# Odd layer of a two-layer transformer step on one core: operand parts on VectorE, gate products between the projections, od norms behind the mLSTM heads, set-up later, folded mean square

## The chip, the cores and the metric

One NeuronCore of a Trainium2 chip runs the whole program. The metric is the device time of one execution in microseconds (us), median of the runs. Engines: PE (TensorE, matrix products), DVE (VectorE), ACT (ScalarE), POOL (GpSimd), SP (SyncE, which issues most DMAs).

## The reference

640 tokens (128 of a prompt, 512 latent) of 1,024 features go through two layers; x stays in float32.

```python
layer(x, cvec, l):                      # l = 0 even, l = 1 odd
    shift, scale, gate = split(silu(cvec) @ ada_w + ada_b, 3)
    h   = rmsnorm(x, norm_g) * (1 + scale) + shift
    out = mix(h) @ w_out                # even: MLA + GQA heads; odd: mLSTM + differential heads
    return x + gate * out

odd mix:  u = h @ w_in  ->  qm, km, vm, om, gates, zm (mLSTM);  qd, kd, vd, gd (differential)
    hm = rmsnorm(sigmoid(om) * (mlstm forward + backward)) * silu(zm)
    od = rmsnorm(attend(q1, k1, v) - lam * attend(q2, k2, v)) * (1 - lam_init) * silu(gd)
    lam = exp(sum(l0 * l1)) - exp(sum(l2 * l3)) + lam_init
y = rmsnorm(x, final_norm_g)            # after the odd layer
```

The keys, values and mLSTM states of the prompt are outputs too.

## The kernel before

The layers run one behind the other; in each, the input projections, the heads and the output projection follow each other in **stages** (us of the profiled execution): even projections 0 to 205, even attention 206 to 375, even output projection with the start of the odd layer 376 to 452, odd projections K, Q, V1 and VM 452 to 553, differential heads 553 to 674, mLSTM heads 674 to 805, output projection and final norm to 871.

**Three products for one.** A product in near float32 is made of three products of rounded operands (`mm3`, L83 to L85): high part times high part, low times high, high times low. Weights come by `wload` (L67): a DMA into `raw` (512 KB, 3 buffers, L75 issued by SP), a cast to the high part `whi` (L76, on ACT unless told otherwise) and a subtraction for the low part `wlo` (L77, on DVE unless told otherwise). `whi` and `wlo` have 2 buffers each.

**The start of the odd layer** (`mid`). The even output projection (`out_proj`) adds its two column halves to x tile by tile, sums squares on ACT (L934), forms 1/rms (L940, L47 on DVE, L48 on POOL) and calls `after` for each of the five token tiles: scale x (L989), transpose (L997, PE), scale and shift half of it on DVE (L1004, h) and half on ACT (L1002), round to `Hh` (L1005, ACT), subtract for `Hl` (L1007: the first half on DVE, the second on POOL). Then projection **V0** (L1027 on: 5 tiles of 24 products 128x272) needs `Hh` and `Hl` of one tile after the other. Its gate columns are `gt` (L1034).

**The projections** K, Q, V1, VM (`odd_linear`): each 120 products (five tiles, eight pieces of the depth, three products). Before them stands the set-up of lambda (L1050 to L1060), behind V1 the mLSTM gates (`mlstm_gates`, L1224 on, with memsets of `pad`, `zz` and `Q`).

**The differential heads** (`diff`): for each of 4 heads and 5 tiles `front` makes two score tiles (L619), row maximum (L626), exp (L629, ACT), and on DVE the factor f (L1174, L1175) and the difference of the two maps (L1176); `back` transposes it (L1188), copies it (L1190) and multiplies by the values (L1195). Between them run, as filler of the PE, the products of `qk_feat` (L1109, eight weight tiles m = 0 to 7, two accumulators), whose casts and low parts are made on POOL, and the eight parts of the odd layer's output gate (`ada_gate_part`: a load into `raw`, L226, eight products L230 that read `raw` itself, and a copy `gp`, L232, ACT). The row of the gate (`ada_gate_row`, L238 to L248, products L241) comes behind mLSTM head 0.

**The order.** The program text gives the dependencies; a scheduler with a simulated timeline fixes each engine's order when the kernel is built, so a change of the text can move instructions far from where it is written. Pools with a fixed number of buffers make an instruction wait until the buffer's last reader is through. `issue_after` keeps instructions behind a given one.

Of the kernel before, what the change touches and what calls it, by code (L numbers as in the profile page):

```python
# [17 lines left out]
EPS = 1e-6  # L18
# [19 lines left out]
class K:  # L38
# [859 lines left out]
    def out_proj(self, W, L, order, gates, otmp, ps, after, tags, then=None):  # L898

        nc = self.nc  # L900
        self.ada_gate_bc(L, gates)
        acc = {t: ps.tile([128, 512], F32, tag=tags[t], name="acc", bufs=5 if tags[t] == "acc" else 1) for t in range(5)}

        def mm(c, t, m, a=0, b=512):
            for k in range(4 * m, 4 * m + 4):
                oh, ol = self.sp[m, t]
                wh, wl = self.ww[c, k // 2]
                self.mm3(acc[t][:, 0:b - a], oh[:, k % 4], ol[:, k % 4], wh[:, k % 2, a:b], wl[:, k % 2, a:b],
                         k == 4 * order[0], k == 4 * order[1] + 3)

        for t in range(5):
            mm(0, t, order[0])
        if order[0] == 0:
            self.op_rest()
        xt = self.xt
        for c in range(2):
            if c:
                for i in range(4):
                    self.op_load(W, 1, (2 * order[0] + i) % 4, i >= 2 and L == "o")
            for t in range(5):  # L920
                parts = [(0, 256), (256, 512)] if then and c and t == 4 else [(0, 512)]
                for i, (a, b) in enumerate(parts):
                    cs, n = slice(c * 512 + a, c * 512 + b), b - a
                    if c:
                        acc[t] = ps.tile([128, 512], F32, tag="acc", name="acc", bufs=5)
                        mm(1, t, order[0], a, b)
                    mm(c, t, order[1], a, b)
                    g = self.gate[:, 1 if t == 0 else 0]
                    tmp = otmp(t + i)[:, 0:n]
                    nc.vector.tensor_tensor(out=tmp, in0=acc[t][:, 0:n], in1=g[:, cs], op=ALU.mult)  # L930
                    eng = nc.gpsimd if L == "e" and c == 0 else nc.vector
                    eng.tensor_tensor(out=xt[:, t, cs], in0=xt[:, t, cs], in1=tmp, op=ALU.add)
                    junk = self.st.tile([128, 512], mybir.dt.bfloat16, tag="sq", name="junk", bufs=1)
                    nc.scalar.activation(out=junk[:, 0:n], in_=xt[:, t, cs], func=AF.Square,  # L934
                                         accum_out=self.sq2[:, c + i, t:t + 1])
                    if then:
                        then(c, t, xt[:, t], cs)
                    if c == 1:
                        ss = self.st.tile([128, 1], F32, tag="ssq", name="ssq", bufs=6)
                        nc.vector.tensor_tensor(out=ss, in0=ss_ if i else self.sq2[:, 0, t:t + 1],  # L940
                                                in1=self.sq2[:, 1 + i, t:t + 1], op=ALU.add)
                        ss_ = ss
                if c == 1:
                    after(t, xt[:, t], self.rsqrt(ss, 1, 1024))


    def odd(self):
# [33 lines left out]
    def mid(self, S, ps):  # L981
# [5 lines left out]
        def after(t, x, r):  # L987
# [4 lines left out]
            for j in range(2):  # L992
# [10 lines left out]
                    else:  # L1003
                        nc.vector.tensor_scalar(out=h32[:, k], in0=src, scalar1=g, scalar2=b, op0=ALU.mult, op1=ALU.add)  # L1004
                nc.scalar.copy(Hh[:, ks, s], h32)  # L1005
                eng = nc.gpsimd if j else nc.vector
                last = eng.tensor_tensor(out=Hl[:, ks, s], in0=h32, in1=Hh[:, ks, s], op=ALU.subtract)  # L1007
                if not j:
                    self.last = last

        def rest():
            for t in range(5):
# [15 lines left out]
        for t in range(5):  # L1028
# [4 lines left out]
            nc.scalar.copy(self.v0[:, t], acc[:, 0:256])  # L1033
            nc.vector.tensor_tensor(out=self.gt[:, t], in0=acc[:, 256:272], in1=self.rows[:, R_GB:R_GB + 16], op=ALU.add)  # L1034

    def odd_linear(self, M, D, Y0, Gp, ps):
        nc, A, O = self.nc, self.A, self.O
        Hh, Hl = self.Hh, self.Hl
# [8 lines left out]
        nc.scalar.dma_start(ck, A["cdkT"])  # L1047
        nc.gpsimd.memset(v1[:, :, :, 128:129], 1.0)

        lam = self.rows[:, R_LAM:R_LAM + 256]  # L1050
        lt = Gp.tile([128, 64], F32, name="lt")
        ls = Gp.tile([128, 2], F32, name="ls")
        for i in range(2):
            nc.vector.tensor_tensor(out=lt, in0=lam[:, 128 * i:128 * i + 64], in1=lam[:, 128 * i + 64:128 * i + 128],
                                    op=ALU.mult)
            nc.vector.tensor_reduce(out=ls[:, i:i + 1], in_=lt, axis=AX.X, op=ALU.add)
        nc.scalar.activation(out=ls, in_=ls, func=AF.Exp)
        self.nlam = nlam = M.tile([128, 1], F32, name="nlam")
        nc.vector.tensor_tensor(out=nlam, in0=ls[:, 1:2], in1=ls[:, 0:1], op=ALU.subtract)
        nc.vector.tensor_scalar(out=nlam, in0=nlam, scalar1=-LAM_INIT, scalar2=None, op0=ALU.add)  # L1060

        vi = lambda t: 5 if t == 0 else t
        for t in range(5):
# [25 lines left out]
        for nm, n, e in (("o_wK", 512, evk), ("o_wQ", 512, evq), ("o_wV1", 256, ev1), ("o_wVM", 512, evv)):  # L1089
            pieces = [(A[nm][i], A[nm].shape[2]) for i in range(A[nm].shape[0])]  # L1090
            if nm == "o_wVM":
                self.head0 = self.prep_dq(0, Y0, ps), self.prep_dk(0, Y0, ps)
            self.lin_tok(pieces, n, Hh, Hl, range(5), e, ps)
            if nm == "o_wV1":
                r = self.mlstm_gates(M, Gp, ps)
        self.gates = r

    def qk_feat(self, ps):

        nc, A = self.nc, self.A  # L1100
        self.qk = self.st.tile([128, 8, 640], F32, tag="ogx", name="qk", bufs=1)
        for m in range(8):
            wh, wl = self.wload(A["o_wkm" if m % 2 else "o_wqm"][m // 2], 8, 128, cp=nc.gpsimd.tensor_copy, lo_on=nc.gpsimd)
            acc = [ps.tile([128, 512], F32, tag="acc", name="acc", bufs=2) for _ in range(2)]
            for k in range(8):
                for a, b, f, l in ((wh, self.Hh, k == 0, False), (wh, self.Hl, False, False),
# [50 lines left out]
    def diff(self, Y0, Y, ps):  # L1157
# [41 lines left out]
        if True:  # L1199
# [4 lines left out]
            for h in range(4):  # L1204
                for t in [1, 2, 3, 4, 0]:
                    cur = front(h, t, qs, ks)
                    if t == 2 and h < 3:
                        nq = self.prep_dq(h + 1, YY[(h + 1) % 2], ps)
                    if t == 3 and h < 3:
                        nk = self.prep_dk(h + 1, YY[(h + 1) % 2], ps)  # L1210
                    if t in (4, 0):
                        self.ada_gate_part("o", 2 * h + (t == 0), ps, "t1", 1)
                    if pend is not None:
                        back(*pend)
                    pend = cur
                qs, ks = nq, nk
# [109 lines left out]
    def mlstm(self, D, ps):  # L1326
# [361 lines left out]
```

## Time and profile before

| | us |
|---|---|
| median of 3 runs (872.51 to 872.6) | 872.58 |
| the profiled execution | 872.72 |
| span of its instructions | 870.9 |
| outside the span | 1.8 |
| PE busy | 830.3 (95%) |
| DVE busy | 532.4 (61%) |
| ACT busy | 425.6 (49%) |
| POOL busy | 249.8 (29%) |

How to read it: the PE is the engine that is nearly always at work, and the mean clock granted to it is 0.996 of the full one. Its instructions are the same before and after the change, so a change of the time shows as idle time of the PE, or as products at the lower clock, in the stage where it arises.

### The profile page before, as it was taken

To read this page: it belongs to the slowest core of one execution; us is meant where nothing else is said; L and a number is where in the kernel's file an instruction comes from. 1 tells how busy PE (TensorE), PEld (TensorE's weight loads), DVE (VectorE), ACT (ScalarE), POOL (GpSimd) and SP (SyncE) were. 2 spreads that over 40 slices of the span, in tenths; PEclk is the share of its full clock that TensorE was granted. 3 is DMA by queue.
4 is the path that set the end of the run, shared out by engine and by line. 5 is a ranking of instruction groups with operands and counts; after the bars stand their busy time and mean duration, and the time that the engine had idled before them with its cause. 6 is when DMAs were issued, how large, how long until landed. Compare 5 with 4: busy or idle time off the path is not lost.

```text
span 870.9 us, 14357 instructions
## 1 busy us (share of the span) xinstructions
PE 830.3 (95%) x5418; PEld 711.2 (82%) x5418; DVE 532.4 (61%) x1143; ACT 425.6 (49%) x936; POOL 249.8 (29%) x240
## 2 busy tenths in 40 slices
PE   5999999999999998899999999999999999999996
PEld 2778899998788766678888898899988788888786
DVE  3674777324766777535751675377674857676845
ACT  5354356423666866623452235456554656533423
POOL 0010241102755766703320000411310833221121
PEclk9999999999999999999999999999999999999999
DMA  9922222221233112554122213122124222153303
GB/s 343 361 74 73 58 81 79 78 85 52 71 105 117 50 49 74 159 210 142 79 85 102 81 54 109 49 82 84 52 75 135 84 68 69 55 175 113 129 2 121
DMA packets 29641, 88.52 MB, mean 102 GB/s; under 512 B 3752, under 2 KB 6880, under 8 KB 29572
## 3 DMA queue, kind: packets, MB, share of 16 engines
q1 hardware_dynamic: 25904, 83.64, 28.3%
q10 hardware_dynamic: 3668, 3.96, 1.4%
q8 instruction: 43, 0.70, 0.3%
q14 instruction: 26, 0.21, 0.1%
HBM read 80.90 MB, written 6.68 MB: 101 GB/s over the span
## 4 chain that ended last, share of the span: by engine, by line
PE 79%; DVE 7%; POOL 5%; ACT 3%; issue 3%; DMA 2%; SPq 0%; POOLq 0%; ACTq 0%; DVEq 0%
PE acc L83 13%; PE acc L85 13%; PE acc L84 13%; PE acc L120 6%; PE s L619 6%; PE acc L1109 6%; PE o L657 3%; PE t L646 3%; PE pv L1516 2%; PE o L1195 2%; PE ada L186 2%; POOL p L639 1%; PE acc L583 1%; DMA raw<-in_o_wO_dram 1%; PE accA L85 1%
## 5 line engine op out<-in xcount | busy, mean ns | idle before, releaser
L84 PE MATMUL acc<-wlo,Hh 128*128 128x512 f32 (+2 forms) x400 | 149.4, 374 | 0.0
L85 PE MATMUL acc<-whi,Hl 128*128 128x512 f32 (+2 forms) x400 | 148.7, 373 | 0.2 <-DVE Hl L1007 0.2
L83 PE MATMUL acc<-whi,Hh 128*128 128x512 f32 (+2 forms) x400 | 145.6, 380 | 2.4 <-ACT Hh L1005 1.4
L77 DVE TENSOR_TENSOR wlo<-raw,whi 128x1024 fp32r<-128x1024 f32 (+4 forms) x67 | 80.1, 1196 | 94.5 <-ACT whi L76 93.9
L76 ACT CAST whi<-raw 128x1024 fp32r<-128x1024 f32 (+4 forms) x71 | 71.7, 1010 | 128.1 <-PE acc L85 76.1
L626 DVE TENSOR_REDUCE nm<-s 128x1 f32<-128x640 f32 (+1 forms) x104 | 81.0, 779 | 52.1 <-PE s L619 51.2
L639 POOL TENSOR_TENSOR p<-p,rs 128x640 f32<-128x640 f32 x64 | 79.2, 1253 | 95.6 <-issue 52.9
L629 ACT ACTIVATE p<-s,nm 128x640 f32<-128x640 f32 (+1 forms) x104 | 79.4, 765 | 38.4 <-DVE nm L626 36.2
L83 PEld LDWEIGHTS acc<-whi,Hh 128*128 128x128 f32 x400 | 75.5, 190 | 14.6 <-ACT Hh L1005 1.7
L85 PEld LDWEIGHTS acc<-whi,Hl 128*128 128x128 f32 x400 | 76.0, 190 | 13.5 <-DVE Hl L1007 0.4
L84 PEld LDWEIGHTS acc<-wlo,Hh 128*128 128x128 f32 x400 | 76.2, 190 | 12.0 <-DVE wlo L77 0.2
L48 POOL TENSOR_TENSOR rs_r<-rs_h,mhalf 128x1 f32<-128x1 f32 (+4 forms) x39 | 36.9, 950 | 148.8 <-DVE rs_h L47 148.5
L646 PE MATMUL t<-cst,p 128*128 128x128 f32 x320 | 46.9, 276 | 3.1 <-POOL p L639 2.2
L85 PE MATMUL acc<-whi,ol 128*128 128x512 f32 (+1 forms) x124 | 48.0, 387 | 0.0
L84 PE MATMUL acc<-wlo,oh 128*128 128x512 f32 (+1 forms) x124 | 47.8, 387 | 0.0
L83 PE MATMUL acc<-whi,oh 128*128 128x512 f32 (+1 forms) x124 | 47.3, 389 | 0.4 <-DVE z L1418 0.4
L646 PEld LDWEIGHTS t<-cst,p 128*128 128x128 f32 x320 | 36.9, 141 | 8.5 <-POOL p L639 3.6
L651 ACT COPY pT<-t 128x512 f32<-128x512 f32 x56 | 32.0, 587 | 19.1 <-PE t L646 18.5
L632 DVE RECIPROCAL rs<-sm 128x1 f32<-128x1 f32 x104 | 16.6, 159 | 27.3 <-ACT p L629 25.7
L619 PE MATMUL s<-Ka,qh 96*128 96x320 f32 (+1 forms) x128 | 31.6, 329 | 1.7 <-DVE og L127 0.9
L1109 PE MATMUL acc<-Hh,whi 128*128 128x320 f32 x128 | 32.5, 323 | 0.5 <-ACT v L1086 0.5
L1148 POOL TENSOR_TENSOR kdl<-ckd,kdh 128x128 fp32r<-128x128 f32 x8 | 3.6, 461 | 100.9 <-ACT kdh L1147 100.9
(385 smaller groups left out, 1925.0 us busy)
## 6 DMA issues: line engine op xcount, KB each, us to landing
adaw<-in_eada_ss_dram SPq DMA_DIRECT2D x16, 512.0 KB
raw<-in_oada_ss_dram SPq DMA_DIRECT2D x16, 512.0 KB
raw<-in_e_wG_dram SPq DMA_DIRECT2D x8, 512.0 KB
raw<-in_eada_g_dram SPq DMA_DIRECT2D x8, 512.0 KB
raw<-in_e_wO_dram SPq DMA_DIRECT2D x8, 512.0 KB
raw<-in_oada_g_dram SPq DMA_DIRECT2D x8, 512.0 KB
raw<-in_o_wO_dram SPq DMA_DIRECT2D x8, 512.0 KB
xT<-in_xT_dram SPq DMA_DIRECT2D x8, 320.0 KB
```

Of the source, the lines that this page charges most:

```text
L76: (cp or nc.scalar.copy)(hi[:, 0:m], raw[:, 0:m])
L77: (lo_on or nc.vector).tensor_tensor(out=lo[:, 0:m], in0=raw[:, 0:m], in1=hi[:, 0:m], op=ALU.subtract)
L83: mm(out, lhsT=lh, rhs=rh, start=first, stop=False)
L84: mm(out, lhsT=lh, rhs=rl, start=False, stop=False)
L85: self.mark = mm(out, lhsT=ll, rhs=rh, start=False, stop=last)
L120: mm(acc[j][:, 0:320], lhsT=a[:, k], rhs=b[:, k, j * 320:j * 320 + 320], start=f, stop=l)
L619: self.mark = self.nc.tensor.matmul(out[:, j, 0:w], lhsT=q[0:rows, qcols], rhs=k[0:rows, a:a + w], start=i == 0, stop=i == len(passes) - 1)
L626: nc.vector.tensor_reduce(out=nm, in_=s, axis=AX.XY, op=ALU.max, negate=True)
L629: nc.scalar.activation(out=p[:, 0:n].rearrange("p (a b) -> p a b", a=s.shape[1]), in_=s, func=AF.Exp, bias=nm, accum_out=sm)
L639: self.pm = self.nc.gpsimd.tensor_tensor(out=p, in0=p, in1=rs.to_broadcast([128, 640]), op=ALU.mult)
L646: self.nc.tensor.transpose(tp[:, i * 128:i * 128 + 128], p[i][:, k * 128:k * 128 + 128], self.ident)
L1109: nc.tensor.matmul(acc[j][:, 0:320], lhsT=a[:, k], rhs=b[:, k, j * 320:j * 320 + 320], start=f, stop=l)
```

## The change

- `out_proj`: the two-step sum of squares and its scaling (L940, L47) become one `scalar_tensor_tensor` with a constant part that is made ahead (`pre`).
- `mid`: all ten low parts `Hl` are subtracted on DVE.
- Lambda (now a function of its own) and `mlstm_gates` are issued behind the last `Hl`, or behind what that name last held.
- `odd_linear`: the eight gate parts leave `diff` and follow the projections: parts 0 and 1 after K, 2 to 4 after Q, 5 after V1, 6 and 7 after VM; they use the `tp` accumulators (3 buffers). The row of the gate follows VM.
- `qk_feat`: the cast goes from POOL to ACT, the low part from POOL to DVE, and each weight tile is asked for one m earlier.
- `mlstm`: the five `unit` calls (rms norm of `od`) leave the start and follow heads 0, 1 and 2.

```diff
@@ out_proj @@
                     if c == 1:
-                        ss = self.st.tile([128, 1], F32, tag="ssq", name="ssq", bufs=6)
-                        nc.vector.tensor_tensor(out=ss, in0=ss_ if i else self.sq2[:, 0, t:t + 1],
-                                                in1=self.sq2[:, 1 + i, t:t + 1], op=ALU.add)
-                        ss_ = ss
+                        ms = self.st.tile([128, 1], F32, tag="rs_h", name="rs_h", bufs=4)
+                        nc.vector.scalar_tensor_tensor(out=ms, in0=self.sq2[:, 1 + i, t:t + 1], scalar=1.0 / 1024,
+                                                       in1=part if i else pre[:, t:t + 1], op0=ALU.mult, op1=ALU.add)
+                        part = ms
                 if c == 1:
-                    after(t, xt[:, t], self.rsqrt(ss, 1, 1024))
+                    r = self.st.tile([128, 1], F32, tag="rs_r", name="rs_r", bufs=6)
+                    nc.gpsimd.tensor_tensor(out=r, in0=ms, in1=self.mhalf[:, 0:1], op=ALU.pow)
+                    after(t, xt[:, t], r)
+            if c == 0:
...
@@ mid, after @@
-                eng = nc.gpsimd if j else nc.vector
-                last = eng.tensor_tensor(out=Hl[:, ks, s], in0=h32, in1=Hh[:, ks, s], op=ALU.subtract)
-                if not j:
-                    self.last = last
+                self.last = nc.vector.tensor_tensor(out=Hl[:, ks, s], in0=h32, in1=Hh[:, ks, s], op=ALU.subtract)
@@ odd_linear @@
-        lam = self.rows[:, R_LAM:R_LAM + 256]
...
+        with self.tc.issue_after(self.last.ins):
+            self.negated_lambda(M, Gp)
@@ odd_linear, the loop over o_wK, o_wQ, o_wV1, o_wVM @@
             self.lin_tok(pieces, n, Hh, Hl, range(5), e, ps)
+            for i in {"o_wK": (0, 1), "o_wQ": (2, 3, 4), "o_wV1": (5,), "o_wVM": (6, 7)}[nm]:
+                self.ada_gate_part("o", i, ps, "tp", 3)
             if nm == "o_wV1":
-                r = self.mlstm_gates(M, Gp, ps)
+                with self.tc.issue_after(self.last.ins):
+                    r = self.mlstm_gates(M, Gp, ps)
+        self.ada_gate_row("o", ps, "tp", 3)
         self.gates = r
@@ qk_feat @@
+        load = lambda m: self.wload(A["o_wkm" if m % 2 else "o_wqm"][m // 2], 8, 128) if m < 8 else None
+        w = load(0)
         for m in range(8):
-            wh, wl = self.wload(A["o_wkm" if m % 2 else "o_wqm"][m // 2], 8, 128, cp=nc.gpsimd.tensor_copy, lo_on=nc.gpsimd)
+            (wh, wl), w = w, load(m + 1)
@@ diff @@
-                    if t in (4, 0):
-                        self.ada_gate_part("o", 2 * h + (t == 0), ps, "t1", 1)
@@ mlstm @@
-        for t in range(5):
-            self.unit(four(od[:, t]))
...
             self.mlstm_head(X2, ps, h, *self.gates, self.v1, hm, ncl, adv)
-            if h == 0:
-                self.ada_gate_row("o", ps, "it", 1)
+            for t in ((0, 1), (2, 3), (4,), ())[h]:
+                self.unit(four(od[:, t]))
```

What the scheduler makes of it, at three places.

**Place 1, between Q and V1.** The DMA queue of SP, before: `raw` buffers are asked for by the weights of K, Q, V1 and VM one behind the other.

```order
L75 DMA raw<-in_o_wK_dram 128x1024
L75 DMA raw<-in_o_wQ_dram 128x1024 x4
L75 DMA raw<-in_o_wV_dram 128x1024 x2
L75 DMA raw<-in_o_wVM_dram 128x1024 x3
L1271 DMA mxd<-Q 36x640
```

The same queue after the change (`oada_g` are the gate parts; `o_wV` with 128x1024 is V1):

```order
L75 DMA raw<-in_o_wK_dram 128x1024
L226 DMA raw<-in_oada_g_dram 128x1024 x2
L75 DMA raw<-in_o_wQ_dram 128x1024 x4
L226 DMA raw<-in_oada_g_dram 128x1024 x3
L75 DMA raw<-in_o_wV_dram 128x1024 x2
L226 DMA raw<-in_oada_g_dram 128x1024
L75 DMA raw<-in_o_wVM_dram 128x1024 x4
```

And the PE after the change, from the last products of Q (128x512) to the first of V1 (128x256):

```order
L84 MATMUL acc<-wlo,Hh_4402 128x512
L85 MATMUL acc<-whi,Hl_4403 128x512
L230 MATMUL gps<-raw,sc 32x128 x24
L83 MATMUL acc<-whi,Hh_4402 128x256 x5
L84 MATMUL acc<-wlo,Hh_4402 128x256
L85 MATMUL acc<-whi,Hl_4403 128x256
```

Three gate loads now stand ahead of V1's first load in the queue, and the 24 products that read these three buffers stand behind the last product of Q.

**Place 2, DVE in the start of the odd layer**, from the last addition of the even output projection (otmp, xt) of tile 4 on. Before (lt: lambda; pad, zz, Q: mLSTM gates):

```order
L1007 TENSOR_TENSOR Hl_4403<-h_4777,Hh_4402 128x4x128
L930 TENSOR_TENSOR otmp<-acc,gate 128x512
L1054 TENSOR_TENSOR lt<-rows 128x64
L1229 MEMSET pad 128x360
L1253 MEMSET zz 36x640
L1255 MEMSET Q 128x1920
L932 TENSOR_TENSOR xt<-xt,otmp 128x512
L1056 TENSOR_REDUCE ls<-lt 128x1
L1004 TENSOR_SCALAR h_4839<-tp,gso 128x128 x4
```

After:

```order
L1012 TENSOR_TENSOR Hl_4403<-h_4773,Hh_4402 128x4x128
L930 TENSOR_TENSOR otmp<-acc,gate 128x512
L1012 TENSOR_TENSOR Hl_4403<-h_4785,Hh_4402 128x4x128
L932 TENSOR_TENSOR xt<-xt,otmp 128x512
L1010 TENSOR_SCALAR h_4833<-tp,gso 128x128 x4
L940 SCALAR_TENSOR_TENSOR rs_h<-sq_77,pre 128x1
L995 TENSOR_SCALAR xt<-xt,rs_r 128x1024
```

Lambda and the memsets are gone from between the two halves of tile 4's addition; one more `Hl` has come in.

**Place 3, ACT at the change from VM to the differential heads**, after the change (v: the evacuations of VM; gp: parts 6 and 7 of the gate; p: the first exps). Before, the five copies v and the first exp were neighbours.

```order
L1094 COPY v_5087<-acc 128x4x128 x3
L76 CAST whi<-raw 128x1024
L232 COPY gp<-gps 128x128 x2
L629 ACTIVATE p,sm<-s_6051,nm 128x640
L629 ACTIVATE p,sm<-s_6069,nm 128x640
L629 ACTIVATE p,sm<-s_6091,nm 128x640
L76 CAST whi<-raw 128x1024
L1127 ACTIVATE qk<-acc 128x320 x2
```

A cast of `qk_feat` and two gate copies stand between them, and the next cast stands ahead of the copies qk that free the accumulators.

## Rows read from the trace of the kernel before

**Rows 1.** The page, first part: busy time of each engine, its share of the span, instructions.

```profile
PE 830.3 (95%) x5418; PEld 711.2 (82%) x5418; DVE 532.4 (61%) x1143; ACT 425.6 (49%) x936; POOL 249.8 (29%) x240
```

**Rows 2.** Busy time by stretch (start:end, length, then PE, PE's weight loads, DVE, ACT, POOL with their instructions, the granted clock, DMA share, GB/s): the projections K to VM; the differential heads with the start of the mLSTM heads.

```profile
450.00:545.00 95.00, 95.00 (x498) 81.31 (x498) 49.95 (x89) 31.35 (x52) 3.60 (x7) 0.99 0.28 93
545.00:690.00 145.00, 139.16 (x1041) 129.60 (x1039) 94.61 (x194) 80.94 (x191) 42.58 (x33) 1.00 0.24 79
```

**Rows 3.** Timeline of the PE in projection V0: start, duration, engine, line, operation, tiles, shape, count; in brackets the idle time before and what ended it. The transposes shown are tile 4's; the last row is the first product of K.

```profile
432.03 0.28 PE L83 MATMUL acc<-whi,Hh 128*128 128x272 f32 x1
432.15 0.29 PE L84 MATMUL acc<-wlo,Hh 128*128 128x272 f32 x1
...
443.94 1.04 PE L997 MATMUL tp<-cst,xt 128*128 128x128 f32 x8
...
447.40 0.39 PE L83 MATMUL acc<-whi,Hh 128*128 128x272 f32 x1 [1.43 <-ACT Hh L1005]
...
452.54 0.63 PE L83 MATMUL acc<-whi,Hh 128*128 128x512 f32 x2
```

**Rows 4.** Busy time by stretch, columns as in rows 2: two stretches of V0 behind its wait, and one in the even attention.

```profile
448.00:450.00 2.00, 1.87 (x9) 1.87 (x10) 0.08 (x1) 0.08 (x1) 2.00 (x5) 0.60 0.00 0
450.00:452.00 2.00, 2.00 (x11) 2.00 (x11) 1.00 (x1) 1.01 (x2) 0.66 (x2) 0.55 0.00 0
350.00:360.00 10.00, 8.25 (x78) 6.62 (x77) 6.43 (x14) 7.05 (x14) 8.03 (x6) 1.00 0.46 131
```

**Rows 5.** Timeline of DVE in the start of the odd layer.

```profile
432.46 1.80 DVE L1007 TENSOR_TENSOR Hl<-h,Hh 128x512 fp32r<-128x512 f32 x1
...
436.39 1.66 DVE L1255 MEMSET Q<- 128x1920 f32 x1 [0.35 <-issue]
437.98 0.62 DVE L932 TENSOR_TENSOR xt<-xt,otmp 128x512 f32<-128x512 f32 x1
...
440.68 0.69 DVE L1007 TENSOR_TENSOR Hl<-h,Hh 128x512 fp32r<-128x512 f32 x1
441.36 0.75 DVE L989 TENSOR_SCALAR xt<-xt,rs_r 128x1024 f32<-128x1024 f32 x1
```

**Rows 6.** Timeline of SP's DMA queue: the two loads of V1.

```profile
483.15 7.86 SPq L75 DMA_DIRECT2D raw<-in_o_wV_dram  x2
```

**Rows 7.** Timeline of the PE in the differential heads: one gate part and the product behind it.

```profile
571.79 0.64 PE L230 MATMUL gps<-raw,sc 128*32 128x128 f32 x16
572.36 0.56 PE L619 MATMUL s<-kdh,q 128*128 128x320 f32 x2
```

**Rows 8.** The chain of waits that ended last, in its stretch ahead of the odd output projection: start, duration, what.

```profile
794.11 4.59 DMA raw<-in_o_wO_dram
...
799.80 1.24 DVE wlo L77
801.06 3.50 DMA raw<-in_o_wO_dram
```

**Rows 9.** Timeline of the PE: instructions that it had to wait for, in the even attention (first row), the differential heads and the start of the mLSTM heads (last row).

```profile
352.73 0.87 PE L619 MATMUL s<-Kb,q 128*128 128x320 f32 x4 [1.75 <-ACT p L629]
...
553.27 0.41 PE L1109 MATMUL acc<-Hh,whi 128*128 128x320 f32 x1 [0.53 <-ACT v L1086]
...
564.85 0.56 PE L619 MATMUL s<-kdh,q 128*128 128x320 f32 x2 [1.02 <-ACT p L629]
...
568.60 0.56 PE L619 MATMUL s<-kdh,q 128*128 128x320 f32 x2 [0.46 <-DVE q L1138]
...
613.71 0.33 PE L1188 MATMUL t<-cst,p 128*128 128x128 f32 x1 [0.43 <-DVE p L1176]
...
631.96 0.63 PE L1188 MATMUL t<-cst,p 128*128 128x128 f32 x4 [0.35 <-DVE p L1176]
...
633.92 0.65 PE L230 MATMUL gps<-raw,sc 128*32 128x128 f32 x16 [1.22 <-ACT pT L1190]
...
674.55 0.50 PE L83 MATMUL acc<-whi,Hh 128*128 128x512 f32 x1 [1.00 <-ACT qk L1113]
...
691.27 0.49 PE L1516 MATMUL pv<-v,s 128*128 128x129 f32 x2 [1.43 <-DVE s L1498]
```

**Rows 10.** Timeline of POOL in the differential heads: one low part of `qk_feat`.

```profile
583.74 2.40 POOL L77 TENSOR_TENSOR wlo<-raw,whi 128x1024 fp32r<-128x1024 f32 x1
```

**Rows 11.** Timeline of DVE at the same time: one factor f.

```profile
584.38 1.77 DVE L1175 SCALAR_TENSOR_TENSOR f<-rs,nlam,f 128x1 f32<-128x1 f32 x1
```

**Rows 12.** The instructions of L1175 in the differential heads: duration in ns, least, median and greatest.

```profile
L1175 DVE SCALAR_TENSOR_TENSOR f<-rs,nlam,f x20: 208/220/1768, 561.4 to 663.6; 128x1 f32<-128x1 f32 x20
```

**Rows 13.** Timeline of ACT: the five evacuations of VM, and the two places where a cast of a weight stood ahead of the copies qk already.

```profile
549.91 3.31 ACT L1086 COPY v<-acc 128x512 f32<-128x512 f32 x5 [9.82 <-PE acc L85]
...
660.24 1.04 ACT L76 CAST whi<-raw 128x1024 fp32r<-128x1024 f32 x1
...
673.12 1.04 ACT L76 CAST whi<-raw 128x1024 fp32r<-128x1024 f32 x1 [2.02 <-PE acc L1109]
```

**Rows 14.** Timeline of POOL at the start of the mLSTM heads: the norm of `od`.

```profile
678.12 1.01 POOL L48 TENSOR_TENSOR rs_r<-rs_h,mhalf 128x4 f32<-128x4 f32 x1
```

**Rows 15.** The end of the chain of waits that ended last.

```profile
865.66 0.17 DVE ssq L940
865.86 0.17 DVE rs_h L47
```

More of the change, by code (lines that the diff above doesn't have):

```diff
@@ L938, in out_proj @@
                     if c == 1:
-                        ss = self.st.tile([128, 1], F32, tag="ssq", name="ssq", bufs=6)
-                        nc.vector.tensor_tensor(out=ss, in0=ss_ if i else self.sq2[:, 0, t:t + 1],
-                                                in1=self.sq2[:, 1 + i, t:t + 1], op=ALU.add)
-                        ss_ = ss
+                        ms = self.st.tile([128, 1], F32, tag="rs_h", name="rs_h", bufs=4)
+                        nc.vector.scalar_tensor_tensor(out=ms, in0=self.sq2[:, 1 + i, t:t + 1], scalar=1.0 / 1024,
+                                                       in1=part if i else pre[:, t:t + 1], op0=ALU.mult, op1=ALU.add)
+                        part = ms
                 if c == 1:
-                    after(t, xt[:, t], self.rsqrt(ss, 1, 1024))
+                    r = self.st.tile([128, 1], F32, tag="rs_r", name="rs_r", bufs=6)
+                    nc.gpsimd.tensor_tensor(out=r, in0=ms, in1=self.mhalf[:, 0:1], op=ALU.pow)
+                    after(t, xt[:, t], r)
+            if c == 0:
+                pre = self.st.tile([128, 5], F32, tag="pre", name="pre", bufs=1)
+                nc.vector.tensor_scalar(out=pre, in0=self.sq2[:, 0], scalar1=1.0 / 1024, scalar2=EPS, op0=ALU.mult,
+                                        op1=ALU.add)
     def odd(self):
@@ L1034, in mid, with negated_lambda @@
             nc.vector.tensor_tensor(out=self.gt[:, t], in0=acc[:, 256:272], in1=self.rows[:, R_GB:R_GB + 16], op=ALU.add)
+    def negated_lambda(self, M, Gp):
+        nc = self.nc
+        lam = self.rows[:, R_LAM:R_LAM + 256]
+        lt = Gp.tile([128, 64], F32, name="lt")
+        ls = Gp.tile([128, 2], F32, name="ls")
+        for i in range(2):
+            nc.vector.tensor_tensor(out=lt, in0=lam[:, 128 * i:128 * i + 64], in1=lam[:, 128 * i + 64:128 * i + 128],
+                                    op=ALU.mult)
+            nc.vector.tensor_reduce(out=ls[:, i:i + 1], in_=lt, axis=AX.X, op=ALU.add)
+        nc.scalar.activation(out=ls, in_=ls, func=AF.Exp)
+        self.nlam = nlam = M.tile([128, 1], F32, name="nlam")
+        nc.vector.tensor_tensor(out=nlam, in0=ls[:, 1:2], in1=ls[:, 0:1], op=ALU.subtract)
+        nc.vector.tensor_scalar(out=nlam, in0=nlam, scalar1=-LAM_INIT, scalar2=None, op0=ALU.add)
     def odd_linear(self, M, D, Y0, Gp, ps):
@@ L1048, in odd_linear @@
         nc.gpsimd.memset(v1[:, :, :, 128:129], 1.0)
-        lam = self.rows[:, R_LAM:R_LAM + 256]
[L1051 to L1060, printed above, removed]
+        with self.tc.issue_after(self.last.ins):
+            self.negated_lambda(M, Gp)
         vi = lambda t: 5 if t == 0 else t
```

## The prediction, written before the change was run

> **What bounds the kernel now.** I read the page's busy times first: the PE works 95% of the span [rows 1]. The change leaves the PE's instructions as they are, so only its idle time and its slow products can change. The stretches came next: between 450 and 545 us the PE is busy 95.00 of 95.00, so the projections wait for nothing; between 545 and 690 it is idle 145 - 139.16 = 5.8 [rows 2]. Then the PE's timeline, gap by gap, told where it waits in the stages that the change touches: once in V0, with products that follow at a lower clock [rows 3, 4], and some eight times in the differential heads and behind them [rows 9]. For each gap I followed the releaser on DVE, ACT and POOL [rows 5, 10, 13], and for each moved instruction which buffer it waits for and who stands behind it in its queue (the three places above).
>
> **The change part by part.** All sums stand against the profiled execution, 872.72; the median of the runs, 872.58, is 0.14 lower, which I neglect.
>
> *V0: -3.6.* Before, the x addition of tile 4 ends late because lambda and a memset of 1.66 stand ahead of it, so that its scaling starts at 441.36 [rows 5] and its transposes at 443.94 [rows 3]. The PE waits 1.43 for `Hh` at 447.40, and the last 24 products of V0, 447.40 to 452.54, take 5.14 where 24 at 0.125, the step at full clock (432.03 to 432.15), would be 3.0 [rows 3]: 2.1 more, most of it the clock, granted at 0.60 and 0.55 in these two stretches [rows 4]. After, nothing foreign stands ahead of the addition; the largest memset alone, 1.66, exceeds the one extra `Hl`, 0.69 beside an idle POOL [rows 5]. Worked through with these durations tile 4's `Hh` and `Hl` are ready 0.8 before the PE comes to them. I take off both the wait and the slow products: -1.43 - 2.1, or -3.6. Bounds: -3.6 and 0 (rival D). That all `Hl` go to DVE costs nothing while DVE keeps ahead; without that cover each would cost its 0.69.
>
> *From Q to V1: +6.3.* Gate products read `raw` themselves, so that each of parts 2, 3 and 4 holds one of the three `raw` buffers until the PE has run it, and the PE runs it behind Q's last product (place 1). V1's first load waits for part 2. Before, V1's loads left at 483.15 and by 491.01 [rows 6], long before their use. After, counted from Q's last product: a gate part takes 0.57 (571.79 to 572.36), its result 0.64 [rows 7]; the load takes 3.50 alone and 4.59 beside others [rows 8], and since three loads leave within 1.2 us I take the middle, 4.05; the cast on ACT takes 1.04 [rows 13]: V1's first product at 5.7. Parts 3 and 4 keep the PE busy until 1.7, so it idles 4.0. Then five products need the high part only (place 1), 0.6, while the low part takes 1.24 [rows 8]: 0.6 more. That is 4.6 (4.0 with the shorter load, 5.1 with the longer).
> To it comes the clock. Behind the wait of 1.43 in V0 the granted clock was 0.60 and 0.55 over two stretches of 2 us, that is the lower level (1.2 GHz instead of 2.4) for nearly all of the time; it cost (0.40 + 0.45) x 2 = 1.7 [rows 4]. Behind the wait of 1.75 at 352.73 it stayed 1.00 [rows 4, 9]. This wait is more than twice as long as either, so I take the nearer row and 1.7; the bounds are 0 and 2.1. The Trainium skill speaks against the change here: "TensorE: Matmul & The Clock Gate", section "HAM oscillation", tells that a wait for a DMA between groups of products puts the array back to the slow clock, so that the next group starts slow. By that rule the term stays 6.3, and without it 4.6; the trace has one wait on either side.
> K to Q and V1 to VM cost nothing: the loads held by parts 0, 1 and 5 are the third and fourth weight piece of the projection behind, needed some 14 us later. If that cover were gone they would cost the same 4.6.
>
> *From VM to the differential heads: +0.5.* The first score waits until the gate's row is summed, which needs the copies gp of parts 6 and 7; on ACT these stand behind the last of the v copies and behind a cast (place 3). The v copies end at 553.22 [rows 13], some 0.7 behind VM's last product; a cast of 1.04 and two short copies bring it to some 2.3. The PE has 2 x 0.57 [rows 7] and 0.2 of other products, so it idles 1.0, where before it idled 0.53 [rows 9]. Bounds: 0 (the scheduler's cast finds ACT free earlier) and +2.2 (the clock falls).
>
> *Differential heads: +0.6.* On the credit side stands POOL. Its low parts of `qk_feat` take 2.40 [rows 10], and while one runs, a DVE subtraction of two values per partition is stretched: f took 1.77 from 584.38 to 586.15, when POOL's low part, begun at 583.74, ended [rows 10, 11]; the median is 0.22 [rows 12]. The PE's waits that I put down to it are 0.46, 0.43, 0.35 and 1.22 (the last for a pT delayed by f) [rows 9]: -2.4. The 1.02 at 564.85 is ACT's and stays.
> On the debit side the eight casts now go to ACT, each 1.04, directly ahead of the copies qk that free the accumulators, at six borders between weight tiles, with the next exp queued behind. Two rows show what such a cast does: at 660.24 the PE had no wait, at 673.12 it waited 1.00 [rows 9, 13]. At the first border ACT is late already (the 1.02), so it pays 1.04 in full; the other five have 1.7 to 2.2 of other PE work in front of them, against 1.04 + 0.77 of ACT, and are nearer to the first row: 0.4 each, 2.0. The gate parts leave, which frees ACT of eight short copies but takes 8 x 0.57 of filler from the PE; I count that as nothing, covered by the next `qk_feat` products, and up to +1.5 without them. Sum -2.4 + 1.0 + 2.0 = +0.6; bounds -2.4 and +3.6 (all six at 1.0), or +5 with the filler.
>
> *Start of the mLSTM heads: -1.0.* A POOL norm of 1.01 [rows 14] no longer stands ahead of a low part of the first head, whose chain ends in the wait of 1.43 at 691.27 [rows 9]. Bounds: 0 and -1.8; the middle. *Tail: -0.2*: of two DVE steps of the last chain, 0.17 each with the step between [rows 15], one is left.
>
> **Sum:** -3.6 + 6.3 + 0.5 + 0.6 - 1.0 - 0.2 = +2.6, or 872.7 + 2.6 = **875.3**. Its own range, from the bounds of the junction and of the casts, is about 872.8 to 878.5.
>
> **The rivals.**
> *B, POOL's release outweighs the casts (not slower).* If all borders are like 660.24, the differential heads give -2.4 instead of +0.6: 875.3 - 3.0 = 872.3, no change; and if the clock holds between Q and V1 as at 352.73, 870.6, faster. It decides at the slack in front of the accumulators' copies: 1.8 of ACT work against 1.7 to 2.2. For it speaks that DVE lost more to POOL than the PE's waits show (20 f of up to 1.77 [rows 12]); against it the first border. The Trainium skill, "SBUF — State Buffer", section "Who interferes with whom", says that a DVE instruction with two SBUF inputs and a GpSimd instruction that reads SBUF exclude each other on a shared port. The row of 1.77 agrees; by that rule every stretched f goes, which is this rival, 872.3.
> *C, the casts cost in full.* All six borders pay 1.0: +3.6 instead of +0.6, 878.3. ACT is busy only 80.94 of 145 [rows 2], which speaks against it, but each exp is on the way to the PE.
> *D, V0 keeps its wait.* If tile 4 is late again, for `Hl` on a DVE that now makes ten, the 3.6 fall out: 878.9. Only 0.8 of margin speaks against it.
> *E, the loads are not held*, the change doing something other than place 1 shows: 875.3 - 6.3 = 869.0. Against it stands the order itself.
>
> **How the numbers follow.** A measurement of this kernel tells about 0.2%, 1.75 us, from no change: faster is below 870.8, slower above 874.3. The forecast has a chance of 0.50 (0.35 slower, 0.15 within), B 0.27 (0.14 within, 0.13 faster), C 0.10 and D 0.08 (slower), E 0.05 (faster). That makes faster 0.18, same 0.29, slower 0.53. The range from 869.6 to 879.6 leaves out E, a little of B, and the outer bounds of C and D.
>
> **What would show it.** Right: V0 without a wait for `Hh` and with a clock of 1.00; between the last 128x512 product of Q and the first 128x256 one a gap of 4 us ended by the cast `whi`, with a granted clock well under 1 behind it; a wait of about 1 us for the gate's sum before the first score; f near its median everywhere; casts on ACT ahead of qk. Wrong: V1's first load leaving before Q's last product, idle time of the PE in the differential heads under 3 or over 8, or a wait for `Hl` in V0.

## The result, and the profile after

| | us |
|---|---|
| before, median of 4 runs | 872.59 |
| changed kernel, median of 4 runs (879.97 to 880.93) | 880.38 |
| ratio to before, 95% interval | 1.0086 (1.0068 to 1.0103) |
| changed kernel, profiled execution / its span | 880.67 / 878.6 |

Slower by 7.8, where 2.6 was forecast with a range up to 879.6.

The page's busy times after (answers to [rows 1]):

```profile
PE 836.1 (95%) x5418; PEld 714.6 (81%) x5418; DVE 534.6 (61%) x1148; ACT 433.6 (49%) x944; POOL 212.7 (24%) x219
```

The span grew by 7.7, the PE's busy time by 5.8 and its idle time by 1.9 only. With the same instructions, longer busy time means slower products.

From Q to V1, the PE's timeline of the changed kernel:

```profile
505.95 0.40 PE L85 MATMUL acc<-whi,Hl 128*128 128x512 f32 x1
506.27 1.52 PE L230 MATMUL gps<-raw,sc 128*32 128x128 f32 x48
511.89 0.86 PE L83 MATMUL acc<-whi,Hh 128*128 128x256 f32 x5 [4.10 <-ACT whi L76]
513.15 0.58 PE L84 MATMUL acc<-wlo,Hh 128*128 128x256 f32 x1 [0.40 <-DVE wlo L77]
```

SP's queue and ACT at the same place:

```profile
481.08 13.96 SPq L226 DMA_DIRECT2D raw<-in_oada_g_dram  x3
506.98 0.80 SPq L75 DMA_DIRECT2D raw<-in_o_wV_dram  x2
```

```profile
510.79 1.04 ACT L76 CAST whi<-raw 128x1024 fp32r<-128x1024 f32 x1 [2.67 <-DMA raw<-in_o_wV_dram]
```

V1's first load leaves behind Q's last product, where before it left at 483.15 [rows 6]; the PE waits 4.10 and 0.40. Stretches of 2 us behind this wait, and two at the first border of the differential heads (columns as in rows 2):

```profile
512.00:514.00 2.00, 1.60 (x9) 1.39 (x10) 2.00 (x3) 1.05 (x1) 0.00 (x0) 0.71 0.29 117
514.00:516.00 2.00, 2.00 (x11) 2.00 (x11) 2.00 (x4) 0.00 (x0) 0.00 (x0) 0.50 0.84 274
516.00:518.00 2.00, 2.00 (x18) 2.00 (x17) 0.80 (x2) 0.00 (x0) 0.00 (x0) 0.94 0.72 240
```

```profile
578.00:580.00 2.00, 2.00 (x10) 2.00 (x10) 1.82 (x4) 0.88 (x2) 0.00 (x0) 0.50 0.13 51
580.00:582.00 2.00, 2.00 (x14) 2.00 (x13) 0.21 (x3) 0.96 (x2) 0.00 (x0) 0.73 0.00 0
```

The granted clock of 0.71, 0.50 and 0.94 costs (0.29 + 0.50 + 0.06) x 2 = 1.7.

V0 as one stretch (answers to [rows 3, 4]): no wait, full clock, 16.8 from its first product to K's where it took 20.5.

```profile
431.90:449.00 17.10, 17.10 (x139) 17.02 (x138) 12.51 (x29) 9.02 (x21) 2.11 (x6) 1.00 0.08 32
```

The PE where VM ends and at the first border of the differential heads (answers to [rows 9]):

```profile
562.24 0.61 PE L241 MATMUL gsum<-gp,cst 128*32 128x256 f32 x6
563.36 0.62 PE L241 MATMUL gsum<-gp,cst 128*32 128x256 f32 x2 [0.52 <-ACT gp L232]
...
576.45 0.56 PE L619 MATMUL s<-kdh,q 128*128 128x320 f32 x2 [1.80 <-ACT p L629]
```

ACT ahead of that border, and the factor f (answers to [rows 12, 13]):

```profile
573.34 1.05 ACT L76 CAST whi<-raw 128x1024 fp32r<-128x1024 f32 x1 [0.34 <-ACT p L629]
574.29 0.76 ACT L1127 ACTIVATE qk<-acc 128x320 f32<-128x320 f32 x2
574.94 0.68 ACT L1151 CAST q<-qtp 64x640 fp32r<-64x640 f32 x1
575.51 0.80 ACT L629 ACTIVATE p<-s,nm 128x640 f32<-128x640 f32 x1
```

```profile
L1189 DVE SCALAR_TENSOR_TENSOR f<-rs,nlam,f x20: 209/219/222, 572.2 to 673.8; 128x1 f32<-128x1 f32 x20
```

f is at its median everywhere, as forecast; the cast stands ahead of the copies qk and the exp that the PE waits for.

What no step had foreseen is seen in a stretch without any wait. Projection K, before and after:

```profile
470.24 0.39 PE L83 MATMUL acc<-whi,Hh 128*128 128x512 f32 x1
470.47 0.39 PE L84 MATMUL acc<-wlo,Hh 128*128 128x512 f32 x1
470.69 0.39 PE L85 MATMUL acc<-whi,Hl 128*128 128x512 f32 x1
470.92 0.39 PE L83 MATMUL acc<-whi,Hh 128*128 128x512 f32 x1
```

```profile
469.98 0.40 PE L83 MATMUL acc<-whi,Hh 128*128 128x512 f32 x1
470.21 0.40 PE L84 MATMUL acc<-wlo,Hh 128*128 128x512 f32 x1
470.45 0.40 PE L85 MATMUL acc<-whi,Hl 128*128 128x512 f32 x1
470.68 0.40 PE L83 MATMUL acc<-whi,Hh 128*128 128x512 f32 x1
```

Three products take 0.68 before and 0.70 after: a step of 0.2267 against 0.2333 at the same granted clock of 1.00. The 360 products of K, Q and VM make 2.4 of it.

One more fall of the clock stands in the even attention, which the change does not touch: here behind a wait of 1.78, where before it stayed at 1.00 behind 1.75 at the same place [rows 4, 9].

```profile
352.00:354.00 2.00, 1.92 (x9) 1.88 (x10) 0.85 (x2) 1.29 (x4) 2.00 (x2) 0.60 0.01 4
354.00:356.00 2.00, 2.00 (x11) 1.72 (x11) 0.90 (x3) 0.92 (x2) 1.83 (x2) 0.55 0.59 156
```

Of the 18 profiles of this document 15 have a fall in this stage; the kernel before, even128 and all256 have none. So the 7.7 of this profile are 1.9 of idle time, 3.4 of clock (1.7 each at the junction, at the first border and here, less V0's 1.7) and 2.4 that are left, as much as the longer steps of K, Q and VM make.

### The profile page after: what moved, and what is told of

Read it like the earlier page. It is cut to its first block, busy times and chain, and to the rows that moved or that the text cites. A ratio compares the mean times of both kernels' runs of the same rounds, so it can differ in the third digit from the quotient of the medians.

```text
span 878.6 us, 14342 instructions
## 1 busy us (share of the span) xinstructions
PE 836.1 (95%) x5418; PEld 714.6 (81%) x5418; DVE 534.6 (61%) x1148; ACT 433.6 (49%) x944; POOL 212.7 (24%) x219
## 4 chain that ended last, share of the span: by engine, by line
PE 82%; DVE 5%; ACT 4%; POOL 3%; DMA 2%; issue 2%; SPq 0%; POOLq 0%; ACTq 0%; DVEq 0%
PE acc L85 14%; PE acc L84 14%; PE acc L83 14%; PE s L619 6%; PE acc L120 6%; PE acc L1123 6%; PE o L657 3%; PE t L646 3%; PE pv L1526 2%; PE o L1209 2%; PE ada L186 2%; POOL p L639 1%; ACT p L629 1%; DVE nm L626 1%; DMA adaw<-in_eada_ss_dram 1%
## 5 line engine op out<-in xcount | busy, mean ns | idle before, releaser
L85 PE MATMUL acc<-whi,Hl 128*128 128x512 f32 (+2 forms) x400 | 150.5, 377 | 0.0
L76 ACT CAST whi<-raw 128x1024 fp32r<-128x1024 f32 (+4 forms) x79 | 80.0, 1013 | 139.7 <-PE acc L85 84.6
L77 DVE TENSOR_TENSOR wlo<-raw,whi 128x1024 fp32r<-128x1024 f32 (+4 forms) x75 | 89.6, 1194 | 93.4 <-ACT whi L76 92.6
L48 POOL TENSOR_TENSOR rs_r<-rs_h,mhalf 128x1 f32<-128x1 f32 (+4 forms) x29 | 29.6, 1029 | 118.4 <-DVE rs_h L47 118.2
L651 ACT COPY pT<-t 128x512 f32<-128x512 f32 x56 | 32.0, 588 | 21.1 <-PE t L646 20.5
L934 ACT ACTIVATE junk<-xt 128x512 bf16<-128x512 f32 (+1 forms) x21 | 12.8, 611 | 42.1 <-DVE xt L932 37.1
```

The costliest lines, as they stand in the source:

```text
L76: (cp or nc.scalar.copy)(hi[:, 0:m], raw[:, 0:m])
L77: (lo_on or nc.vector).tensor_tensor(out=lo[:, 0:m], in0=raw[:, 0:m], in1=hi[:, 0:m], op=ALU.subtract)
L85: self.mark = mm(out, lhsT=ll, rhs=rh, start=False, stop=last)
```

## The experiments

Ratios are to the kernel before on the same chip, with their intervals; a difference of two ratios times 872.6 is given in us. By the intervals such a difference is good to about 2 us either way.

**The junction and the parts alone.** `a_two`: two gate parts behind Q.

```diff
-            for i in {"o_wK": (0, 1), "o_wQ": (2, 3, 4), "o_wV1": (5,), "o_wVM": (6, 7)}[nm]:
+            for i in {"o_wK": (0, 1), "o_wQ": (2, 3), "o_wV1": (4, 5), "o_wVM": (6, 7)}[nm]:
```

> The changed kernel with two gate parts behind Q and two behind V1 instead of three and one, so that one raw buffer stays free for V1's first load. Theory (the load is held): the wait of 4.10 and the one of 0.40 at V1's start go, and with them the slow clock behind them (1.7), 880.4 - 6.2 = 874.2. Rival (the PE then waits elsewhere in the projections, or V1's second load takes its place): 878 or more. Whether products 128x512 in K to VM step at 0.233 us, as in the changed kernel, or at 0.227, as before, is read from the same trace: 0.233 would say that the gate loads' number has nothing to do with it.

874.5, ratio 1.0025 (1.0010 to 1.0041): 5.3 less than the changed kernel (5.9 by the medians). SP's queue and the PE at the junction of this kernel:

```profile
495.09 7.33 SPq L75 DMA_DIRECT2D raw<-in_o_wV_dram  x2
```

```profile
506.65 1.08 PE L230 MATMUL gps<-raw,sc 128*32 128x128 f32 x32
507.66 0.39 PE L83 MATMUL acc<-whi,Hh 128*128 128x256 f32 x1
```

V1's load leaves at 495.09 and no wait is left: the held load is shown as the cause. K still steps at 0.233.

`a_qkpool` (the changed kernel) and `b_qkact` (the kernel before): the qk_feat part undone, and done alone.

```diff
-        load = lambda m: self.wload(A["o_wkm" if m % 2 else "o_wqm"][m // 2], 8, 128) if m < 8 else None
-        w = load(0)
         for m in range(8):
-            (wh, wl), w = w, load(m + 1)
+            wh, wl = self.wload(A["o_wkm" if m % 2 else "o_wqm"][m // 2], 8, 128, cp=nc.gpsimd.tensor_copy, lo_on=nc.gpsimd)
```

> The changed kernel with the casts and low parts of qk_feat back on POOL, loads asked for as before. Theory (ACT's casts at the borders between weight tiles cost more than POOL's hold on DVE): the wait of 1.80 at the first border falls back to about 1.0, its slow clock (1.7) goes, f is stretched again; 880.4 - 3.0 = 877.4. Rival (POOL's hold on DVE is as dear): 880.4, no difference; or dearer: 881 to 883.

> The kernel before with the casts of qk_feat on ScalarE and its low parts on VectorE, loads one weight tile earlier, and nothing else changed. Theory: the first border's wait grows from 1.0 to 1.8 and the clock falls behind it, other borders cost a little, f is at its median: 872.6 + 1.5 to 3.0 = 874.1 to 875.6. Rival (freeing VectorE from POOL is worth more): 872.6 - 2.4 = 870.2.

a_qkpool 1.0077 (1.0057 to 1.0097), 0.8 less than the changed kernel, and b_qkact 1.0004 (0.9989 to 1.0020): neither is clear of no difference. The first border's wait is 1.02 in the one and 1.80 in the other:

```profile
575.71 0.56 PE L619 MATMUL s<-kdh,q 128*128 128x320 f32 x2 [1.02 <-ACT p L629]
566.06 0.56 PE L619 MATMUL s<-kdh,q 128*128 128x320 f32 x2 [1.80 <-ACT p L629]
```

From VM's last product to the first of the mLSTM heads, the kernel before and b_qkact (columns as in rows 2):

```profile
552.45:674.56 122.11, 116.42 (x940) 110.87 (x938) 80.63 (x178) 68.53 (x169) 25.70 (x18) 1.00 0.24 81
552.86:675.42 122.56, 116.81 (x939) 111.13 (x937) 84.01 (x185) 75.46 (x176) 1.85 (x4) 1.00 0.25 80
```

The clock is full in both, and the stage is 0.45 longer, which the noise of the runs hides. b_qkact kept V0's wait, and told something else. Its PE at that wait, and the stretches behind:

```profile
449.36 0.39 PE L83 MATMUL acc<-whi,Hh 128*128 128x272 f32 x1 [1.43 <-ACT Hh L1005]
```

```profile
450.00:452.00 2.00, 1.91 (x15) 1.91 (x16) 0.03 (x1) 0.72 (x1) 2.00 (x5) 1.00 0.00 0
452.00:454.00 2.00, 2.00 (x14) 1.78 (x14) 1.64 (x3) 1.65 (x3) 0.82 (x3) 1.00 0.00 0
```

Behind the same wait of 1.43 the clock stays at 1.00 here (and in `b_shift`, below), where it fell to 0.60 and 0.55 in the execution of [rows 4]. V0 takes 19.0 in these two, 20.5 there, and 16.8 without the wait.

`b_v0`: the start of the odd layer alone (its three edits of the diff, on the kernel before).

> The kernel before with the start of the odd layer alone changed: all low parts Hl on VectorE, lambda and the mLSTM gates behind them, folded mean square. Theory: V0 loses its wait and its slow clock, 872.6 - 3.7 = 868.9, and the gap-free projections behind it stay as they were. Rival (the longer step of the products, 0.233 instead of 0.227 us in K, Q and VM, comes with this part): 360 x 0.0066 = 2.4 is given back, 871.3.

0.9997 (0.9983 to 1.0011). V0 took 16.8, so its gain was there, but K, Q and VM stepped at 0.2333, as the rival said. The part that brings the longer step is this one.

**The address.** The build's allocation shows one difference in front of `Hh`: the new tile `pre` moves `Hh`, `Hl` and, in the same place later, `os` by 32 bytes. `b_shift` does that alone; `a_align`, `a_two_align` (with a_two) and `v0_align` (b_v0) undo it.

```diff
# b_shift
+            nc.gpsimd.memset(M.tile([128, 8], F32, name="shift"), 0.0)
             self.Hh = Hh = M.tile([128, 8, 640], F32R, tag="Hh1", name="Hh1", bufs=1)
# the three others
-                pre = self.st.tile([128, 5], F32, tag="pre", name="pre", bufs=1)
-                nc.vector.tensor_scalar(out=pre, in0=self.sq2[:, 0], scalar1=1.0 / 1024, scalar2=EPS, op0=ALU.mult,
+                pre = self.sq2[:, 0]
+                nc.vector.tensor_scalar(out=pre, in0=pre, scalar1=1.0 / 1024, scalar2=EPS, op0=ALU.mult,
                                         op1=ALU.add)
```

> The kernel before with one unused tile of 32 bytes per partition in front of Hh, as the changed kernel has one (pre), so that Hh, Hl and os start at 0 instead of 32 in 64 bytes while the weights' parts stay at 32. Nothing else is changed. Theory (a product 128x512 whose two operands start at different halves of 64 bytes steps at 0.2333 instead of 0.2267 us): K, Q and VM 360 x 0.0067 = +2.4, the fillers and the output projection of the mLSTM stage another 0 to 2.3, as far as they set the pace: 874.9 to 877.2, and K at 0.2333 in the trace. Rival (the step comes with the order of the instructions): 872.5 and 0.2267.

> The changed kernel with pre written in place into sq2, so that the new tile and its 32 bytes go and Hh, Hl and os start where they did before. Theory (operands at different halves of 64 bytes): K, Q and VM at 0.2267 again, 880.4 - 2.4 to 4.7 = 875.7 to 878.0. Rival (the step comes with the order): 880.4 and 0.2333.

> Two gate parts behind Q, and pre in place: both costs taken away. Theory: the two add up, 874.5 - 2.4 to 4.7 = 869.8 to 872.1, no slower than before. Rival (no address effect): 874.5.

> The kernel before with the start of the odd layer alone changed (as b_v0), and pre in place. Theory: b_v0 showed no gain since the longer step gave it back; 872.4 - 2.4 to 4.7 = 867.7 to 870.0, with V0 at 16.8 and K at 0.2267. Rival (V0's gain is not real, or is given back elsewhere): 872.4.

b_shift 1.0033 (1.0020 to 1.0046), +2.9, for 32 unused bytes; a_align 1.0054 (1.0040 to 1.0068), -2.8 from the changed kernel; a_two_align 0.9992 (0.9976 to 1.0008), -2.9 from a_two; v0_align 0.9968 (0.9957 to 0.9980), -2.5 from b_v0. K in b_shift, then in a_align, the first and the fourth of four products in a row:

```profile
469.68 0.40 PE L83 MATMUL acc<-whi,Hh 128*128 128x512 f32 x1
...
470.38 0.40 PE L83 MATMUL acc<-whi,Hh 128*128 128x512 f32 x1
```

```profile
469.69 0.39 PE L83 MATMUL acc<-whi,Hh 128*128 128x512 f32 x1
...
470.37 0.39 PE L83 MATMUL acc<-whi,Hh 128*128 128x512 f32 x1
```

0.70 and 0.68 for three: the address, not the order. `v0_full`, `even128`, `all128` and `all256` asked which part of the address, on products that the change does not touch: v0_align with 32 or 96 unused bytes ahead of the right-hand pool's other tiles; the last two also with 64 or 192 in front of the second operands of the even output projection (pool S), and with the od norms moved.

```diff
+            nc.gpsimd.memset(self.C.tile([128, 24], F32, name="shiftC"), 0.0)    # v0_full: 8
             self.rows = self.C.tile([128, NROW], F32, name="rows")
...
+                nc.gpsimd.memset(S.tile([128, 48], F32, name="shiftS"), 0.0)     # all256; all128: 16
                 self.mid(S, ps)
```

> The kernel v0_align with one unused tile of 32 bytes at the head of the right-hand pool, so that 240 products 128x512 of the even projections and 120 of the even output projection, whose operands lay in different halves of 64 bytes, lie in the same half; 36 products of another projection go the other way. Theory (address): 0.2267 instead of 0.2333 us there, 324 x 0.0067 = -2.2 from 871.0, so 868.8. Rival (the even projections step at 0.2333 for another reason): 871.0.

> The kernel v0_align with one unused tile of 96 bytes (v0_full: 32) at the head of the right-hand pool, so that Hh and Hl of the even projections start at 32 in 128 bytes as their weights do (v0_full: 96 against 32, equal in 64 but not in 128). Theory (the step depends on the operands' starts in 128 bytes): the even projections, 240 products, step at 0.2267 for the first time, -1.6 from v0_align, and the even output projection's second half stays at 0.2333. Rival (it was 64 bytes, and the even projections are slow for another reason): 0.2333 there, no gain.

> even128 with another 64 unused bytes in front of the even output projection's second operands, so that these lie alike too, and with the od norms behind the mLSTM heads (as full_units). Theory (128 bytes): even projections and even output projection all at 0.2267, -1.6 from full_units (869.0), so 867.4. Rival: 869.0.

> all128 with 192 instead of 64 unused bytes in front of the even output projection's second operands: in all128 that half stayed at 0.233 with starts of 160 and 32 in 256 bytes, equal in 128. Theory (the step depends on the starts in 256 bytes): the whole even output projection at 0.2267, 120 x 0.0067 = -0.8 from all128 (868.1), 867.3. Rival (another cause in that half): 868.1 and 0.233.

| products 128x512 | kernel | starts in 256 bytes: weights, tokens | step |
|---|---|---|---|
| K, Q, VM | before | 160, 160 | 0.227 |
| K, Q, VM | changed, b_shift | 160, 192 | 0.233 |
| even projections | before / v0_full / even128 | 160, 0 / 160, 224 / 160, 160 | 0.233 / 0.233 / 0.227 |
| even output projection, second half | before / changed | 0, 224 / 0, 0 | 0.233 / 0.227 |
| the same | all128 / all256 | 160, 32 / 160, 160 | 0.232 / 0.227 |

The even projections, v0_full and even128, again the first and the fourth product:

```profile
84.19 0.39 PE L83 MATMUL acc<-whi,Hh 128*128 128x512 f32 x1
...
84.89 0.39 PE L83 MATMUL acc<-whi,Hh 128*128 128x512 f32 x1
```

```profile
83.73 0.39 PE L83 MATMUL acc<-whi,Hh 128*128 128x512 f32 x1
...
84.41 0.39 PE L83 MATMUL acc<-whi,Hh 128*128 128x512 f32 x1
```

The second half of the even output projection, all128 (14 steps in 3.25) and all256 (15 steps in 3.40):

```profile
388.38 0.40 PE L83 MATMUL acc<-whi,oh 128*128 128x512 f32 x1
...
391.63 0.40 PE L85 MATMUL acc<-whi,ol 128*128 128x512 f32 x1
```

```profile
388.27 0.39 PE L83 MATMUL acc<-whi,oh 128*128 128x512 f32 x1
...
391.67 0.39 PE L83 MATMUL acc<-whi,oh 128*128 128x512 f32 x1
```

Both of my narrower theories (64, then 128 bytes) fell; equal starts in 256 bytes fit every row of the table. They are not shown for all products: in the odd output projection of the kernel before, those with starts of 224 and 160 stepped at 0.233 in some stretches and at 0.230 in others, and no run tells why. Ratios: v0_full 0.9961 (0.9947 to 0.9974), even128 0.9960 (0.9945 to 0.9975), all128 0.9944 (0.9927 to 0.9961), all256 0.9944 (0.9923 to 0.9966), median 866.9: the best version, 5 below before. The ratios are too coarse to tell these four apart, and it is the trace that does: the even output projection takes 58.0 in all128 and 57.3 in all256.

**The rest.** `full_units` (v0_full with the od norms moved), `full_units_qkm` (with only the low parts of qk_feat on DVE), `v0_gates` (v0_align with the gate parts two by two and the row behind VM), `all256_qkact` (all256 with the qk_feat part).

> v0_full with the norms of od behind the mLSTM heads, as the changed kernel has them. Theory (a POOL norm leaves the head of the first mLSTM head's chain): the wait of 1.1 to 1.4 for s at the start of the mLSTM heads goes, -1.0 from v0_full. Rival (the scheduler had them where they cost nothing): no difference.

> full_units with the low parts of qk_feat on VectorE while their casts stay on POOL. Theory (it is ACT's casts at the borders that cost, and POOL's low parts of 2.4 that hold DVE): no wait of 1.8 at the first border, and the waits of 0.3 to 1.2 behind POOL's low parts go: -1.0 to -2.4 from full_units. Rival (a low part on DVE, 1.2, at the border costs as much as it saves): no difference.

> v0_align with the eight gate parts between the projections, two behind each, and the gate's row behind VM; nothing else of the change. Theory (only the row's wait of some 0.5 at the start of the differential heads and the filler taken from them cost): 871.0 + 0.5 to 1.5. Rival (the filler's loss exposes the score chain): 871.0 + 2 to 4.

> all256 with the qk_feat part of the change (casts on ScalarE, low parts on VectorE). Theory (the first border's wait grows from 1.0 to 1.8, others shrink): +0.5 to +1.5 from all256. Rival (freeing VectorE is worth more): -1 to -2.

full_units 0.9959 (0.9944 to 0.9973): the wait of 1.43 for s is 0.32, -0.2 from v0_full by the ratios and -0.6 by the medians, not clear of the interval. The wait in v0_full, then in full_units:

```profile
689.70 0.49 PE L1526 MATMUL pv<-v,s 128*128 128x129 f32 x2 [1.43 <-DVE s L1508]
688.39 0.49 PE L1526 MATMUL pv<-v,s 128*128 128x129 f32 x2 [0.32 <-DVE s L1508]
```

In the profiles the mLSTM heads, up to the output projection, take 130.9 and 129.8. full_units_qkm 0.9966 (0.9953 to 0.9979) gained nothing: its f is at most 0.221, but its differential heads take 123.05 against 122.10 in full_units.

v0_gates 0.9998 (0.9984 to 1.0011): +2.6 from v0_align. The stage from VM's last product to the first of the mLSTM heads in v0_align, then in v0_gates, and in v0_gates the products of the row, which wait for nothing, and one wait of the stage:

```profile
551.64:673.75 122.11, 116.41 (x939) 110.83 (x937) 80.62 (x178) 68.64 (x169) 25.73 (x18) 1.00 0.25 81
556.27:677.54 121.27, 114.91 (x852) 110.82 (x851) 80.27 (x179) 66.91 (x163) 26.07 (x18) 0.99 0.16 55
```

```profile
557.25 1.19 PE L241 MATMUL gsum<-gp,cst 128*32 128x256 f32 x8
...
636.89 1.94 PE L1207 MATMUL o<-vd,pT 128*128 128x128 f32 x10 [1.28 <-ACT pT L1202]
```

all256_qkact 0.9945 (0.9927 to 0.9963): +0.1 from all256, which meets neither expectation; the PE's idle time in the differential heads is alike, 5.74 with the casts on ACT and 5.68 with POOL's low parts.

## Why the prediction was wrong

- **The step that failed** is the first: "only its idle time and its slow products can change", where slow meant the clock (as in "How to read it" ahead of it). The change also moved the tiles. 648 products more than before have operands that start differently in 256 bytes (720 of K, Q, VM and the mLSTM fillers and 48 of the output projection, less 120 of the even output projection that came to lie alike), at most 648 x 0.0067 = 4.3; moving the tiles alone cost 2.9 (1.7 to 4.0), undoing it gave 2.5 to 2.9. 875.3 + 2.9 = 878.2 lies within the range; the 2.2 up to 880.4 are in the terms below, the gate parts above all.
- **Q to V1: right.** 6.3 forecast; 4.10 + 0.40 + 1.7 = 6.2 in the profile, 5.3 to 5.9 by a_two (and 5.4 between a_align and a_two_align). In all three profiles that have this wait (4.10, 4.64 in a_qkpool, 4.66 in a_align) the clock falls. The Trainium skill, "TensorE: Matmul & The Clock Gate", section "HAM oscillation", has a wait for a DMA between groups of products put the array back to the slow clock; the trace agrees at this wait, with 0.71, 0.50 and 0.94 behind it.
- **V0: the mechanism right, the size that of one execution.** -3.6 forecast, -2.8 (-3.8 to -1.7) in v0_align, an interval that holds 3.6 too. The wait went in every profile with this part. The clock's 1.7 can be had back only in executions where it had fallen, and b_qkact and b_shift show two where it had not: there V0 would lose 2.2, not 3.7. I had read one execution's clock as the kernel's.
- **Gates and their row: mis-sized.** +0.5 forecast at VM's end, where the wait is 0.52 against 0.53 before, and v0_gates has none; yet v0_gates is 2.6 slower. As far as the profiles show, the term that failed is the filler taken from the differential heads, which the prediction counted "as nothing". v0_gates' profile is 3.9 longer than v0_align's: 1.7 is a fall of the clock behind the wait of 1.28 (a_qkpool has the same wait and a fall), and the PE's idle time grew from 5.70 to 6.36 in the differential heads and from 2.13 to 2.53 in the mLSTM heads, which had lost the row. What makes the other 1.1, and how often the clock falls there, stays open.
- **Differential heads: as forecast in the profiles, too small for the runs to show.** +0.6 forecast; 0.1 to 0.8 by the three kernels, none clear of no difference, and 0.45 and 0.48 by the stage in the profiles of before and b_qkact, all256 and all256_qkact. In the changed kernel's one profile the fall of the clock behind the wait of 1.80 adds 1.7; b_qkact has that wait at the full clock. Rival B had its mechanism, with f at most 0.222, but not its gain: the four waits put down to POOL, 2.46 together, shrink to 0.62 in b_qkact, and new ones behind ACT take their place. The casts are not all of it, since full_units_qkm, without them, gained nothing either. That f is no longer stretched agrees with the Trainium skill, "SBUF — State Buffer", section "Who interferes with whom", by which a DVE instruction with two inputs in SBUF and a GpSimd instruction that reads SBUF get in each other's way.
- **mLSTM start: -1.0 forecast**, the wait went from 1.43 to 0.32 and the stage of the profile is 1.1 shorter; the runs gave 0.2 to 0.6, which is not clear of nothing.

Sum of what was measured alone: 5.3 + 2.9 - 2.8 + 2.6 + 0.1 - 0.2 = 7.9, against 7.5 by the ratio. With terms that are each good to 1 to 2 us, it is in part luck that the sum comes this close.

## What to carry to other kernels

A small tile added in front of large operands changes where these lie; when products slow down with a full clock and no wait, compare the step of equal products and the addresses of both operands. Loading into a buffer that a late reader holds blocks every load behind it, so count the buffers that moved readers hold at each junction against those that the next stage's first load needs. A fall of the clock seen in one execution is a chance, not a term.

## What the runs showed of the hardware

- In the projections and the even output projection of the table, a product of 128x128 by 128x512 in fp32r stepped at 0.2267 us where both operands started alike in 256 bytes and at 0.232 to 0.2333 where they did not, at a granted clock of 1.00. Products of 128x272 (0.125) and 128x320 (0.147) showed no such difference between before and after.
- Behind one and the same wait the granted clock stays at 1.00 in one execution and falls in another: V0's 1.43 (1.00 and 0.55), the even attention's 1.75 and 1.78 (1.00 and 0.55). A fall cost 1.7 us at the places read, and 3.4 behind the wait of 4.66 in a_align (0.62, 0.50, 0.50 and 0.68 in four stretches of 2 us).
